# Layer 1's MLP weight sums made during layer 0's MLP, three units behind the norm, and an earlier first down block

## Chip, cores and metric

One Trainium2 chip, one core of it. The metric is the device time of one execution in microseconds (us).

## What is computed

A two-layer diffusion backbone over 1024 latent tokens and 256 context tokens, D_MODEL 1024, D_FF 4096, in float32. Layer 0 mixes with a bidirectional mLSTM and a Fourier transform, layer 1 with differential attention and a convolution. Each layer ends with the part that the change touches:

```python
def squared_relu_mlp(h, w1, w2):
    return jnp.square(jax.nn.relu(h @ w1)) @ w2
...
        x = x + mod_l[2] * y_l
        x = x + mod_l[5] * squared_relu_mlp(modulate(rmsnorm(x, g_norm[l, 1]), mod_l[3], mod_l[4]), w_ff1[l], w_ff2[l])
```

Layer 0 runs the MLP on latent and context tokens, layer 1 on the latent tokens alone.

## The kernel before

**Arithmetic.** A float32 product is made of three matmuls: each operand is split into a rounded half `hi` and a rest `lo`. ACT makes `hi` (a cast), DVE makes `lo` (a subtraction). Weights come through a ring of three staging tiles `st` (128x1024 floats, 512 KB): SP loads one (L95), ACT casts it to `wah` or `wbh` (L108), DVE subtracts to `wal` or `wbl` (L109), and the tile is free again.

**Layer 0's MLP** (`mlp`, L728). The hidden size is done in blocks of three 128-wide hidden tiles. A block is an up phase (three tiles by three token blocks, `acc`, then Relu, Square and a split, L747 to L751) and a down phase (eight output tiles `fo` by three token blocks, `ff`, each added to the residual `x` by DVE at L708, with four banks for `ff`). Six weight loads feed a block, three of `ff1` and three of `ff2`. Beside the down phase runs `side`: layer 1's modulation vectors, made by DVE (L179, L181) from loads of `w_mod`, five or six to a block, through the same three `st` tiles.

**Layer 1's MLP** uses a seven-product scheme for 2x2 block matrices in place of eight products. Products are named by WORDER "1","5","6","3","7","2","4". The right-hand operands `B` are made from the normed activations behind the norm (`right1`, L1194): sums and differences by DVE and POOL, then a split. The left-hand operands are sums and differences of weight quarters. `left` (L1215) loads two `st` tiles, and makes the sums with four 128x512 additions on POOL for the up products (L1240 to L1244) and on DVE for the down products, then splits them (ACT L1224, DVE L1225). An up unit (`up_unit`, L1312) is 84 matmuls (seven products by four operand pairs by three) and covers two hidden tiles; there are 16. What the products give is gathered in four tiles of a ring `x` of eight (L1321 keeps a product, L1328 adds one). Units 0 to 13 store the right-hand operands of the down products to DRAM (`sw`), five of seven already split (NSPLIT 5); units 14 and 15 store plain tiles to `sd`. The first products "1" and "2" need only the unsummed half of the operands; units 0, 1 and 2 run them before and behind the norm's own matmuls, then `together` (L1300) interleaves units 0 and 1 for products 5, 6, 3, 7, 4, and unit 2 follows. The down products take the units' results in five blocks (DBLK, three units each, two in the last) by four pairs of output tiles. They begin after all 16 residual tiles `x` are reloaded from DRAM (L1127) and the first block's operands are loaded from `sw` (L1382, L1385).

**Order.** The kernel is written in this order, and a scheduler moves instructions within each engine's list. Each engine, SP's DMA queue among them, works through its list in order: an instruction that waits holds up all that stands behind it.

## Time and profile before

| | us |
|---|---|
| median of 3 runs (range) | 3122.47 (3122.32 to 3123.63) |
| profiled execution | 3123.65 |
| its span, first to last instruction | 3121.9 |
| PE busy | 2940.3 (94%) |
| DVE busy | 1997.1 (64%) |
| ACT busy | 1203.9 (39%) |
| POOL busy | 222.8 (7%) |
| DMA engines, mean rate | 120 GB/s |

The profiled execution took 1.75 us more than its span, and 1.18 us more than the median. The mean granted TensorE clock was 0.978 of full speed. Shares of a whole span hide stages with different limits, so stretches are read one by one below. Line numbers are those of the kernel before; the changed kernel has the same statements some lines later (L710 for L708, L111 for L109, L1311 for L1268).

### The profile page before, as it was taken

To read this page: it belongs to the slowest core of one execution; us is meant where nothing else is said; L and a number is where in the kernel's file an instruction comes from. 1 tells how busy PE (TensorE), PEld (TensorE's weight loads), DVE (VectorE), ACT (ScalarE), POOL (GpSimd) and SP (SyncE) were. 2 spreads that over 40 slices of the span, in tenths; PEclk is the share of its full clock that TensorE was granted. 3 is DMA by queue.
4 is the path that set the end of the run, shared out by engine and by line. 5 is a ranking of instruction groups with operands and counts; after the bars stand their busy time and mean duration, and the time that the engine had idled before them with its cause. 6 is when DMAs were issued, how large, how long until landed. Compare 5 with 4: busy or idle time off the path is not lost. (4 is left out here: it accounts for less than half of the span.)

```text
span 3121.9 us, 44126 instructions
## 1 busy us (share of the span) xinstructions
PE 2940.3 (94%) x16386; PEld 2463.2 (79%) x16386; DVE 1997.1 (64%) x3957; ACT 1203.9 (39%) x2660; POOL 222.8 (7%) x315
## 2 busy tenths in 40 slices
PE   6899999999999999999999798999999699969998
PEld 5787878788888888888888677877877577758787
DVE  5858696646454544444456687566677976647787
ACT  3335354433222222222242155566665545422222
POOL 0002011000000000000000000000001432300000
PEclk9999999999999999999999899999999899989999
DMA  6143334550122222222121433134432355585652
GB/s 213 45 154 111 110 112 140 179 166 28 41 75 75 82 68 81 82 68 75 55 84 54 140 97 104 58 96 126 157 98 102 134 210 206 202 298 177 235 170 75
DMA packets 231911, 373.22 MB, mean 120 GB/s; under 512 B 21536, under 2 KB 116368, under 8 KB 231696
## 3 DMA queue, kind: packets, MB, share of 16 engines
q1 hardware_dynamic: 229104, 366.47, 35.8%
q10 hardware_dynamic: 2592, 3.93, 0.4%
q8 instruction: 129, 2.11, 0.3%
q14 instruction: 86, 0.70, 0.1%
HBM read 283.95 MB, written 86.37 MB: 119 GB/s over the span
## 5 line engine op out<-in xcount | busy, mean ns | idle before, releaser
L127 PE MATMUL acc<-a,wah 128*128 128x512 f32 (+1 forms) x1736 | 642.3, 370 | 14.9 <-DVE rt L1000 14.2
L128 PE MATMUL acc<-a,wah 128*128 128x512 f32 (+1 forms) x1736 | 637.5, 367 | 0.0
L129 PE MATMUL acc<-a,wal 128*128 128x512 f32 (+1 forms) x1736 | 636.7, 367 | 0.0
L127 PEld LDWEIGHTS acc<-a,wah 128*128 128x128 f32 x1736 | 332.5, 192 | 61.4 <-DVE rt L1000 14.8
L129 PEld LDWEIGHTS acc<-a,wal 128*128 128x128 f32 x1736 | 332.2, 191 | 46.3 <-DVE wal L109 0.2
L128 PEld LDWEIGHTS acc<-a,wah 128*128 128x128 f32 x1736 | 332.6, 192 | 45.1 <-issue 0.5
L127 PE MATMUL ff<-s,wbh 128*128 128x512 f32 (+1 forms) x768 | 274.0, 359 | 0.0
L108 ACT CAST wah<-st 128x1024 fp32r<-128x1024 f32 (+4 forms) x121 | 117.2, 971 | 404.1 <-DMA st<-in_ff_dram 305.2
L128 PE MATMUL ff<-s,wbh 128*128 128x512 f32 (+1 forms) x768 | 272.3, 355 | 0.0
L129 PE MATMUL ff<-s,wbl 128*128 128x512 f32 (+1 forms) x768 | 271.6, 354 | 0.0
L708 DVE SCALAR_TENSOR_TENSOR x<-ff,mod,x 128x512 f32<-128x512 f32 (+1 forms) x264 | 173.3, 660 | 105.4 <-PE ff L129 103.4
L751 DVE TENSOR_TENSOR s<-s,s 128x512 fp32r<-128x512 f32 (+1 forms) x96 | 57.9, 603 | 285.0 <-ACT s L750 284.9
L109 DVE TENSOR_TENSOR wal<-st,wah 128x1024 fp32r<-128x1024 f32 (+4 forms) x121 | 135.4, 1121 | 117.8 <-ACT wah L108 117.8
L1050 DVE TENSOR_REDUCE mx<-S 128x1 f32<-128x512 f32 (+1 forms) x288 | 165.8, 595 | 69.1 <-PE S L1048 67.4
L1268 PE MATMUL bd<-a,wbh 128*128 128x512 f32 x480 | 153.5, 400 | 43.3 <-ACT wbh L1224 23.5
L1056 ACT ACTIVATE p<-S,nm 128x512 f32<-128x512 f32 (+1 forms) x288 | 176.1, 620 | 44.2 <-DVE nm L1053 43.9
L1048 PE MATMUL S<-K,Q 128*128 128x512 f32 (+1 forms) x576 | 163.5, 383 | 14.0 <-ACT p L1056 7.6
L127 PE MATMUL acc<-wah,a 128*128 128x256 f32 (+1 forms) x560 | 163.1, 292 | 6.9 <-ACT a L269 4.5
L127 PEld LDWEIGHTS ff<-s,wbh 128*128 128x128 f32 x768 | 144.8, 189 | 23.6 <-ACT s L750 0.4
L128 PEld LDWEIGHTS ff<-s,wbh 128*128 128x128 f32 x768 | 145.2, 189 | 20.6 <-issue 0.2
L129 PEld LDWEIGHTS ff<-s,wbl 128*128 128x128 f32 x768 | 144.9, 189 | 20.8
L128 PE MATMUL acc<-wal,a 128*128 128x256 f32 (+1 forms) x560 | 160.7, 288 | 0.0
(395 smaller groups left out, 5924.6 us busy)
## 6 DMA issues: line engine op xcount, KB each, us to landing
st<-in_ff_dram SPq DMA_DIRECT2D x103, 512.0 KB
a<-sw SPq DMA_DIRECT2D x112, 256.0 KB
st<-in_w_mod_dram SPq DMA_DIRECT2D x48, 512.0 KB
sw<-o SPq DMA_DIRECT2D x70, 256.0 KB
stm<-in_w_mod_dram SPq DMA_DIRECT2D x128, 128.0 KB
bc<-rb SPq DMA_DIRECT2D x30, 512.0 KB
sw<-x SPq DMA_DIRECT2D x56, 256.0 KB
st<-in_w_qk_dram SPq DMA_DIRECT2D x24, 512.0 KB
```

The lines of the kernel that those rows point to most:

```text
L108: act.copy(hi, v)
L109: dve.tensor_sub(lo, v, f(hi))
L127: pe.matmul(ps, lh, rh, start=first, stop=False)
L128: pe.matmul(ps, lh, rl, start=False, stop=False)
L129: pe.matmul(ps, ll, rh, start=False, stop=last)
L708: dve.scalar_tensor_tensor(xt, ps, mod[:, self.l, ch, fo, s:s + 1], xt, MUL, ADD)
L751: dve.tensor_sub(lo, r, f(hi))
L1048: pe.matmul(s_, Q[m][:, kind, qb * P:(qb + 1) * P], K[hh, m][:, a:a + n], start=(kind == 0), stop=(kind == 1))
L1050: dve.tensor_reduce(mx[:, i:i + 1], s_, AX, MAX)
L1056: act.activation(e[:, a:a + n], S[i], AF.Exp, bias=nm, accum_out=Z[:, m, i:i + 1])
L1268: pe.matmul(ps, l_, r_, start=bool(first) and j == 0 and i == 0, stop=j == n - 1 and i == 2, skip_group_check=True)
```

## The change

- **Sums.** A generator `wsums` makes all weight sums of layer 1 while layer 0's MLP runs: 60 steps, two at each `fo` of the down phases, so 16 to a block of the first three middle blocks and 12 in the fourth. A step loads two halves of 256 KB into an `st` tile, adds and subtracts in place with four dependent 128x256 operations on POOL, and stores 512 KB to DRAM, `su` for `ff1` (32 steps) or `sv` for `ff2` (28 steps).
- **Left operands.** `left` makes no sums. It loads seven quarter operands, four of them sums, and splits them: 1.75 MB to an up unit.
- **Three units.** Units 1 and 2 are made inside the last loop of the attention output projection (`out_part`), at `fo` 2 and 5, and `together` interleaves three units. `out_part` takes its weights through `wa` instead of `wb`.
- **Down.** NSPLIT goes from 5 to 3, so two more of seven operands are split when they are read and not when they are stored. The first down block has two units, not the last. The last up unit takes the product order LORDER; behind its products "2" and "6" the first block's operands are loaded, and behind "4" four residual tiles. The other residual tiles are reloaded pair by pair of output tiles (`reload_x`), and the next block's operands are issued at the last pair of a block.

```diff
-DBLK = ((0, 1, 2), (3, 4, 5), (6, 7, 8), (9, 10, 11), (12, 13))
+DBLK = ((0, 1), (2, 3, 4), (5, 6, 7), (8, 9, 10), (11, 12, 13))
 NWP = 14
 WORDER = ("1", "5", "6", "3", "7", "2", "4")
-NSPLIT = 5
+LORDER = ("1", "2", "6", "7", "4", "5", "3")
+NSPLIT = 3
+NO = 21
...
+                for _ in range(2):
+                    next(sums, None)
...
+    su = dram.tile([16, P, 4, KT // 2, P], F32, name="su")
+    sv = dram.tile([NWP, 2, P, 2, 2, 2, P], F32, name="sv")
...
+        def wsums():
+            for j in range(16):
+                for h in (0, 1):
+                    t = wp.tile([P, 1024], F32, tag="st", bufs=3, name="st")
+                    v = t.rearrange("p (i e n c) -> p i e n c", i=2, e=2, c=P)
+                    for i in (0, 1):
+                        sp.dma_start(v[:, i], A["ff1"][1, 2 * j + i].rearrange("p (e n) c -> p e n c", e=2)[
+                            :, :, 2 * h:2 * h + 2])
+                    wsum(v)
+                    sp.dma_start(su[j, :, :, 2 * h:2 * h + 2], t.rearrange("p (s n c) -> p s n c", s=4, c=P))
+                    yield
+            for j in range(NWP):
+                for h in (0, 1):
+                    t = wp.tile([P, 1024], F32, tag="st", bufs=3, name="st")
+                    for e in (0, 1):
+                        sp.dma_start(t[:, e * 512:e * 512 + 512], A["ff2"][1, 2 * j + e, :, h * 512:h * 512 + 512])
+                    wsum(t.rearrange("p (e n i c) -> p i e n c", e=2, i=2, c=P))
+                    sp.dma_start(sv[j, h], t.rearrange("p (e n i c) -> p e n i c", e=2, i=2, c=P))
+                    yield
+        def wsum(v):
+            a, b, c, d = v[:, 0, 0], v[:, 0, 1], v[:, 1, 0], v[:, 1, 1]
+            pool.tensor_add(d, c, d)
+            pool.tensor_sub(c, a, c)
+            pool.tensor_sub(a, d, a)
+            pool.tensor_sub(b, b, a)
...
+        def ops_of(qs, pl, tag, stage):
+            e = len(qs)
+            v = four(stage(), e)
+            for i, q in enumerate(qs):
+                load(q, v[:, i])
+            hi, lo = (four(pl.tile([P, 1024], F32R, tag=tag + x, bufs=3, name=tag + x), e) for x in "hl")
...
         ops = {}
-        f0 = raw(0)
-        ops["1"], ops["2"] = split(f0, wp, "wa")
+        ops["1"], ops["2"] = ops_of(("A11", "A12"), wp, "wa", st)
+        if not early:
+            yield ops
+        ops["5"], ops["6"] = ops_of(("S1", "S2"), pfw, "wb", ws)
+        if early:
+            yield ops
+        ops["3"], = ops_of(("S4",), pfw, "wb", st)
+        ops["7"], ops["4"] = ops_of(("S3", "A22"), wp, "wa", st)
         yield ops
-        if again:
-            f0 = raw(0)
-        f1, y = raw(1), four(pf.tile([P, 1024], F32, tag="ws", bufs=1, name="ws"))
-        eng.tensor_add(y[:, 0], f1[:, 0], f1[:, 1])
-        eng.tensor_sub(y[:, 1], y[:, 0], f0[:, 0])
-        ops["5"], ops["6"] = split(y, pfw, "wb")
-        eng.tensor_sub(f1[:, 0], f0[:, 0], f1[:, 0])
-        eng.tensor_sub(f0[:, 1], f0[:, 1], y[:, 1])
-        ops["3"], = split(f0[:, 1:2], pfw, "wb")
-        ops["7"], ops["4"] = split(f1, wp, "wa")
-        yield ops
-
-    def up_left(j, again):
-        def load(i, t):
-            sp.dma_start(t, A["ff1"][1, 2 * j + i].rearrange("p (e n) c -> p e n c", e=2))
-        return left(load, HK, pool, again)
+
...
-        out_part(fo, 1, 6, KT, pfw, "wb")
+        out_part(fo, 1, 6, KT)
         spill(fo, 1)
+        if fo in (2, 5):
+            lead.append(up_unit(len(lead), True))
     norm_later(res.tot[1], 512, res.bank, right1)
-    for j in (1, 2):
-        lead.append(up_unit(j, True))
-        lead[j].run("1", "2")
+    for u in lead[1:]:
+        u.run("1", "2")
     drain()
     for op in "56374":
-        together(lead[:2], op)
-    for u in lead[:2]:
+        together(lead, op)
+    for u in lead:
         u.store()
-    lead[2].run(*"56374")
-    lead[2].store()
-    for j in range(3, 16):
+    for j in range(3, 15):
         u = up_unit(j)
         u.run(*WORDER)
         u.store()
-    load_x(px, 0, "x", F32, x2)
-    load_x(ap_, 1, "a2", F32R, x2)
-    for blk in DBLK:
-        B = down_ops(blk)
+    u = up_unit(15, False, LORDER)
+    nxt = {}
+    for op in LORDER:
+        u.run(op)
+        if op == "2":
+            nxt.update(down_ops(DBLK[0], ("1", "5", "6", "3")))
+        elif op == "6":
+            d = down_unit(DBLK[0], 0, nxt)
+            nxt.update(down_ops(DBLK[0], ("7", "2", "4")))
+        elif op == "4":
+            reload_x(0)
+    u.store()
+    for i, blk in enumerate(DBLK):
+        right, nxt = nxt, {}
         for fo in range(0, KT, 2):
-            down_unit(blk, fo).run(*WORDER)
+            if i or fo:
+                d = down_unit(blk, fo, right)
+            if i == 0 and fo < KT - 2:
+                reload_x(fo + 2)
+            if fo == KT - 2 and i + 1 < len(DBLK):
+                nxt = down_ops(DBLK[i + 1])
+            d.run(*WORDER)
...
+    def reload_x(fo):
+        for k, tb in ((fo, 0), (fo + 1, 1), (fo, 1), (fo + 1, 0)):
+            pl, t, dt = (ap_, "a2", F32R) if tb else (px, "x", F32)
+            res.x[k, tb] = f(pl.tile([P, 512], dt, tag=t, bufs=8, name=t))
+            sp.dma_start(res.x[k, tb], x2[:, k, tb * 512:tb * 512 + 512])
```

SP's queue in a down phase of layer 0's MLP, before (`in_w_mod` are modulation loads, `in_ff1` and `in_ff2` the next block's weights):

```order
L95 DMA st_9260<-in_w_mod_dram 128x4x256
L95 DMA st_9303<-in_w_mod_dram 128x4x256
L95 DMA st_9342<-in_ff1_dram 128x1024
L95 DMA st_9348<-in_ff2_dram 128x1024
L95 DMA st_9449<-in_ff1_dram 128x1024
```

and in the changed kernel, the last four of a block's 16 sums:

```order
L97 DMA st_9358<-in_w_mod_dram 128x4x256
L887 DMA st_9366<-in_ff1_dram 128x2x256 x2
L887 DMA st_9374<-in_ff1_dram 128x2x256 x2
L890 DMA su_7097<-st_9366 512x1x256
L890 DMA su_7097<-st_9374 512x1x256
L97 DMA st_9417<-in_w_mod_dram 128x4x256
L887 DMA st_9423<-in_ff1_dram 128x2x256 x2
L887 DMA st_9431<-in_ff1_dram 128x2x256 x2
L890 DMA su_7097<-st_9423 512x1x256
L890 DMA su_7097<-st_9431 512x1x256
L97 DMA st_9472<-in_ff1_dram 128x1024
L97 DMA st_9478<-in_ff2_dram 128x1024
```

All 16 sums of a block, and its modulation loads, now stand in front of the next block's first weight load.

DVE at the end of that block, before (L109 makes the `lo` half of the next block's weights, L708 updates the residual):

```order
L708 SCALAR_TENSOR_TENSOR x_7317<-ff_9268,mod,x_7317 128x512
L181 SCALAR_TENSOR_TENSOR av<-st,sT,av 128x256
L109 TENSOR_TENSOR wal<-st,wah 128x1024
L708 SCALAR_TENSOR_TENSOR x_7325<-ff_9279,mod,x_7325 128x512
L708 SCALAR_TENSOR_TENSOR x_7333<-ff_9290,mod,x_7333 128x256
```

and in the changed kernel, where these are the block's last updates:

```order
L710 SCALAR_TENSOR_TENSOR x_7320<-ff_9439,mod,x_7320 128x512
L710 SCALAR_TENSOR_TENSOR x_7328<-ff_9450,mod,x_7328 128x512
L710 SCALAR_TENSOR_TENSOR x_7336<-ff_9461,mod,x_7336 128x256
L192 STREAM_TRANSPOSE sc<-lone 128x64
L194 TENSOR_TENSOR mod<-sc,vec 128x2 x2
L111 TENSOR_TENSOR wal<-st,wah 128x1024
L111 TENSOR_TENSOR wbl<-st,wbh 128x1024
L111 TENSOR_TENSOR wal<-st,wah 128x1024
```

Before, this split stood among the updates of the last output tile but one, and another three tiles further ahead; at the ends of three blocks all six splits now stand behind the last update.

PE behind layer 1's second norm, before (product "5" writes `bd`, product "6" `acc`; `a_23152` and `a_23164` are the first and last operand of "5"):

```order
L1268 MATMUL bd<-a_23164,wbl 128x512
L1268 MATMUL acc<-o,wbh 128x512 x2
L1268 MATMUL bd<-a_23152,wbh 128x512
L1268 MATMUL bd<-a_23153,wbh 128x512
L1268 MATMUL acc<-o,wbl 128x512
```

and in the changed kernel (`a_23658` is the first operand of "5"):

```order
L1311 MATMUL bd<-a_23670,wbl 128x512
L1311 MATMUL acc<-o,wbh 128x512 x2
L1311 MATMUL bd<-a_23658,wbh 128x512
L1311 MATMUL bd<-a_23659,wbh 128x512
L1311 MATMUL bd<-a_23658,wbl 128x512
L1311 MATMUL bd<-a_23658,wbh 128x512
L1311 MATMUL bd<-a_23659,wbh 128x512
L1311 MATMUL bd<-a_23658,wbl 128x512
```

Behind unit 0's product "5" and the first pair of its "6", which has to wait for its operand, the same operand of "5" now serves two more units instead of one.

## Rows read from the trace of the kernel before

**Rows 1.** Busy table by stretch: layer 0's MLP, up and down, then layer 1's MLP.
```profile
core 0: us, PE busy (x) PEld busy (x) DVE busy (x) ACT busy (x) POOL busy (x), PEclk, DMA share, GB/s
801.27:842.60 41.33, 41.33 (x218) 35.67 (x217) 12.07 (x22) 14.83 (x26) 0.00 (x0) 1.00 0.17 52
...
926.90:969.60 42.70, 42.70 (x257) 36.43 (x250) 33.20 (x77) 4.03 (x6) 0.00 (x0) 1.00 0.28 87
...
2405.50:2477.00 71.50, 47.92 (x181) 35.05 (x181) 62.84 (x70) 31.47 (x49) 37.14 (x24) 0.83 0.27 95
2477.00:2762.80 285.80, 272.44 (x1161) 216.89 (x1159) 188.19 (x245) 135.44 (x221) 77.85 (x49) 0.99 0.63 227
2762.80:2786.30 23.50, 0.03 (x1) 0.03 (x1) 6.61 (x12) 3.44 (x7) 0.00 (x0) 0.57 1.04 351
2786.30:3061.00 274.70, 271.87 (x1169) 219.49 (x1169) 211.20 (x325) 74.81 (x112) 0.00 (x0) 0.99 0.58 189
```

**Rows 2.** Waits of PE between 2380 and 3061 us: total, times, longest.
```profile
PE bd L1268 <- ACT wbh L1224: 23.5, 1, 23.5
PE acc L1268 <- ACT x L1321: 15.2, 11, 6.9
PE bd L1268 <- ACT a L1174: 9.5, 1, 9.5
```

**Rows 3.** Timeline, SP's DMA issues from 790 us: start, length, engine, line, count.
```profile
792.37 19.02 SPq L95 DMA_DIRECT2D st<-in_w_mod_dram  x5
```

**Rows 4.** Timeline, SP's DMA issues from 862 us: weight loads of the next block.
```profile
862.62 6.15 SPq L95 DMA_DIRECT2D st<-in_ff_dram  x2
```

**Rows 5.** Timeline, ACT from 862 us: the cast of the first of those loads.
```profile
866.09 1.05 ACT L108 CAST wah<-st 128x1024 fp32r<-128x1024 f32 x1 [22.03 <-DMA st<-in_ff_dram]
```

**Rows 6.** Groups of DVE by line in one block of layer 0's MLP, 801 to 885 us.
```profile
L181 DVE SCALAR_TENSOR_TENSOR av<-st,sT,av 128x256 f32<-128x256 f32 x19 | 9.1, 480 | 1.8 <-DMA st<-in_w_mod_dram 1.8
L751 DVE TENSOR_TENSOR s<-s,s 128x512 fp32r<-128x512 f32 (+1 forms) x9 | 5.4, 603 | 28.8 <-ACT s L750 28.8
L109 DVE TENSOR_TENSOR wal<-st,wah 128x1024 fp32r<-128x1024 f32 x2 | 2.5, 1226 | 0.3 <-ACT wah L108 0.3
```

**Rows 7.** Groups of POOL by line in layer 1's MLP, 2380 to 3061 us.
```profile
L1244 POOL TENSOR_TENSOR st<-st,ws 128x512 f32<-128x512 f32 x16 | 33.2, 2075 | 74.3 <-DVE wal L1225 52.5 <-ACT o L1365 21.8
L1243 POOL TENSOR_TENSOR st<-st 128x512 f32<-128x512 f32 x16 | 22.9, 1431 | 0.0
```

**Rows 8.** Groups of POOL by line, whole span: the one of 128x256.
```profile
L621 POOL TENSOR_SCALAR_AFFINE_SELECT E<-E 128x256 f32<-128x256 f32 x60 | 26.1, 458 | 108.5 <-ACT E L619 92.6 <-PE pu L589 15.7
```

**Rows 9.** Timeline of POOL, 2418 to 2447 us.
```profile
2426.14 2.27 POOL L1241 TENSOR_TENSOR ws<-ws,st 128x512 f32<-128x512 f32 x1
2428.37 1.27 POOL L1243 TENSOR_TENSOR st<-st 128x512 f32<-128x512 f32 x1
...
2443.03 3.38 POOL L1212 TENSOR_TENSOR x<-x 128x512 f32<-128x512 f32 x2
```

**Rows 10.** Timeline of DVE, 2440 to 2450 us.
```profile
2443.54 1.75 DVE L1178 SCALAR_TENSOR_TENSOR a<-a,mod,a 128x512 fp32r<-128x512 f32 x1
...
2448.74 0.74 DVE L1178 SCALAR_TENSOR_TENSOR a<-a,mod,a 128x512 fp32r<-128x512 f32 x1
```

**Rows 11.** Timeline of ACT, 2418 to 2447 us.
```profile
2428.44 1.04 ACT L1224 CAST wbh<-ws 128x1024 fp32r<-128x1024 f32 x1 [7.76 <-POOL ws L1241]
```

**Rows 12.** Timeline of PE, 2418 to 2447 us.
```profile
2430.06 0.80 PE L1268 MATMUL bd<-a,wbh 128*128 128x512 f32 x1 [9.51 <-ACT a L1174]
...
2444.35 1.22 PE L1268 MATMUL acc<-o,wbh 128*128 128x512 f32 x2 [6.88 <-ACT x L1321]
```

**Rows 13.** Timeline, SP's DMA issues where the down products start.
```profile
2762.41 3.45 SPq L1127 DMA_DIRECT2D x<-x  x7
...
2770.62 4.41 SPq L1382 DMA_DIRECT2D a<-sw  x7
...
2778.15 2.32 SPq L1259 DMA_DIRECT2D st<-in_ff_dram  x4
```

More of the change, by code (lines that the diff above doesn't have):

```diff
@@ L726, in norm2, with mlp @@
             norm_later(self.tot[tb], TBS[tb][1], self.bank, sink)
-    def mlp(res, pf, pw, p2, tbs, h2, segs, finish, pre, lead, side):
+    def mlp(res, pf, pw, p2, tbs, h2, segs, finish, pre, lead, side, sums):
         l = res.l
@@ L1203, in right1 @@
             dve.tensor_sub(x[k, 0], x[k + HK, 1], x[k, 0])
-        B["6"] = [osplit(po_, "o", 20, x[k, 0], shift(k + HK)) for k in range(HK)]
+        B["6"] = [osplit(po_, "o", NO, x[k, 0], shift(k + HK)) for k in range(HK)]
         B["3"] = [osplit(ap_, "a5", 32, x[k + HK, 1], shift(k + HK)) for k in range(HK)]
@@ L1209, in right1 @@
             pool.tensor_sub(x[k, 1], x[k + HK, 1], x[k, 1])
-        B["7"] = [osplit(po_, "o", 20, x[k, 1], db[:, k:k + 1]) for k in range(HK)]
+        B["7"] = [osplit(po_, "o", NO, x[k, 1], db[:, k:k + 1]) for k in range(HK)]
         for k in range(HK):
@@ L1213, in right1, with left, four @@
         B["4"] = [osplit(ap_, "a2", 8, x[k + HK, 0]) for k in range(HK)]
-    def left(load, n, eng, again=False):
-        def four(t):
-            return t[:, :2 * n * P].rearrange("p (e n c) -> p e n c", e=2, c=P)
-        def split(v, pl, tag):
-            e = v.shape[1]
-            hi, lo = (four(pl.tile([P, 1024], F32R, tag=tag + x, bufs=3, name=tag + x))[:, 0:e] for x in "hl")
+    def left(load, n, early=False):
+        def four(t, e):
+            return t[:, :e * n * P].rearrange("p (e n c) -> p e n c", e=e, c=P)
+        def ops_of(qs, pl, tag, stage):
[4 more added lines that the diff above has]
+            hi, lo = (four(pl.tile([P, 1024], F32R, tag=tag + x, bufs=3, name=tag + x), e) for x in "hl")
             act.copy(hi, v)
@@ L1226, in split, with st, ws @@
             return [(hi[:, i], lo[:, i]) for i in range(e)]
-        def raw(i):
-            t = four(wp.tile([P, 1024], F32, tag="st", bufs=3, name="st"))
-            load(i, t)
-            return t
+        def st():
+            return wp.tile([P, 1024], F32, tag="st", bufs=3, name="st")
+        def ws():
+            return pf.tile([P, 1024], F32, tag="ws", bufs=1, name="ws")
         ops = {}
-        f0 = raw(0)
-        ops["1"], ops["2"] = split(f0, wp, "wa")
-        yield ops
-        if again:
-            f0 = raw(0)
@@ L1254, in down_left @@
-    def down_left(blk, fo):
-        n, h = len(blk), 2 * blk[0]
-        def load(i, t):
-            for e in range(2):
-                sp.dma_start(t[:, e], A["ff2"][1, h + e:h + 2 * n:2, :, (fo + i) * P:(fo + i + 1) * P].rearrange(
-                    "h p c -> p h c"))
-        return left(load, n, dve)
+        ops["1"], ops["2"] = ops_of(("A11", "A12"), wp, "wa", st)
[4 more added lines that the diff above has]
+            yield ops
@@ new lines, in left, with up_left, load @@
+        ops["3"], = ops_of(("S4",), pfw, "wb", st)
+        ops["7"], ops["4"] = ops_of(("S3", "A22"), wp, "wa", st)
+        yield ops
+    SUMS = ("S2", "S4", "S3", "S1")
+    def up_left(j, early):
+        def load(q, t):
+            if q in SUMS:
+                src = su[j, :, SUMS.index(q)]
+            else:
+                src = A["ff1"][1, 2 * j + int(q[1]) - 1].rearrange("p (e n) c -> p e n c", e=2)[:, int(q[2]) - 1]
+            sp.dma_start(t, src)
+        return left(load, HK, early)
@@ L1296, in run @@
                 ps, first = self.bank(op)
-                product(ps, op, self.A, B, first)
+                product(ps, op, self.A, self.right, first)
                 self.finish(op, ps)
@@ L1307, in together, with up_unit @@
             for u, (ps, first) in zip(units, banks):
-                product(ps, op, u.A, B, first, (j,))
+                product(ps, op, u.A, u.right, first, (j,))
         for u, (ps, _) in zip(units, banks):
             u.finish(op, ps)
-    def up_unit(j, again=False):
+    def up_unit(j, early=False, order=WORDER):
         t = {}
@@ L1388, in down_ops, with down_unit @@
         return nb
-    def down_unit(blk, fo):
+    def down_unit(blk, fo, right):
         def upd(*to):
```

33 lines of the change are left out of this document (22 added, 11 removed).

## The prediction

> **What bounds the kernel now.** I read the page first: PE is busy 94% of the span, so a gain has to come from PE's idle time or from stretches at the lower of its two clocks (1.2 of 2.4 GHz), and a loss from making PE idle where it is not. So the second view is the busy table by stretch [rows 1]. In layer 0's MLP, where the sums go, PE is busy in all of every stretch, at full clock; POOL does nothing there, the DMA engines are 17 to 28% busy. That is the room the change counts on, and PE has no slack to give. An up phase of 41.33 us is 216 matmuls, 72 for each of the token blocks of 512, 512 and 256, or 180 of 512 in all: 0.2296 us for one. Up and down together make 84 us to a block.
>
> In layer 1's MLP three stretches lose time. Behind the norm (2405.5 to 2477) 181 matmuls should take 41.6 us and took 71.5: 30 us lost. The units up to 2762.8 are 1152 matmuls by the code (60 of unit 2, 13 units of 84), 264.5 us, and took 285.8: 21 us. The start of the down products is 23.5 us without a matmul, and the down products' 1176 matmuls, 270.0 us, took 274.7. Together 79 us: no more than this can be won. The list of PE's waits [rows 2] names them: one of 23.5 us for ACT's cast of the first down weights, one of 9.5 for a split operand of product "5", eleven of 15.2 in all for ACT's copy L1321.
>
> **What the sums cost in layer 0.** What limits them is not POOL's time but three staging tiles and SP's order: 16 sums stand in front of the next block's weights. Step by step:
> - A load: weights issued at 862.62 were cast at 866.09, so 3.5 us from issue to use [rows 4, 5]. A sum's load comes in two halves, the second issued 0.4 us after the first (an issue takes 0.5 to 0.6 by lengths and counts in [rows 13], with the DMA engines full; I take a little less): 3.9. A store of the same size is given 3.5.
> - A POOL operation: the nearest of its kind is 128x512 [rows 7, 9], 1.27 us at its shortest, 1.43 on average at L1243. Half the width halves the 1.27 to 0.64; what the mean lies above the least, 0.16, I leave whole, since it is waiting and not width. Dependent ones follow without a gap, as L1243 does with no idle time in front of it [rows 7]. 0.80 us, so 3.2 us to a sum. Ends: 0.46 us, the one POOL row of 128x256, with one input in place of two [rows 8], and 1.04, half of L1244's 2.08.
> - A round: two sums are loaded, POOL takes 3.2 us for each in turn, the second store is issued (0.4 us) and the next loads stand behind it; the first store, issued at 7.1, has landed by 10.6. The third tile goes to modulation loads. 3.9 + 6.4 + 0.4 = 10.7 us for two sums, 86 for 16.
> - Six weight loads through three tiles: two passes of 3.5, a cast of 1.05 [rows 5] and three splits of 1.23 [rows 6], 8.2 each, 16.
> - 102 us against 84: 18 us late in each of three blocks, 54. The fourth has 12 sums, 64 + 16 = 80, and is not late.
> - The lead: the first modulation load of this phase goes out at 792.37 [rows 3], 9 us ahead of the up phase at 801.27 [rows 1]. Less 9.
> - Three stalls of several us let the granted clock fall, as it did behind the norm, where the stretch with the long waits has a mean of 0.83 [rows 1]: 3 us, an estimate.
>
> **Layer 0 loses 48 us.** PE shows it at two places: in front of the next block's first product, since all six splits stand behind the block's last update, and inside the down phase, since DVE's modulation steps [rows 6] wait for loads that now stand behind sums, and the residual updates that free the four `ff` banks stand behind those steps.
>
> POOL and DVE hold each other up: L1178 took 1.75 us while POOL was at work and 0.74 a few us later; L1241 took 2.27 us where L1243 took 1.27 [rows 9, 10]. The Trainium skill speaks against the change here: "GPSIMD Engine Reference", section "Key points", says that GpSimd shares its SBUF interfaces with VectorE and contends with DVE instructions that have two SBUF inputs. By that rule the modulation steps and weight splits of [rows 6] would be held up beside the sums; the trace agrees as far as L1178 goes.
>
> **What layer 1 gains.**
> - Behind the norm. ACT's cast for product "5" stood behind a cast of weights that waited for POOL's sum until 2428.4 [rows 9, 11]; without that sum "5" starts 2 us earlier than 2430.06 [rows 12], at 2428. It then has three units to serve, 36 matmuls, 8.3 us, some of it at half clock: 2439. Product "6" waited until 2444.35 for a free tile of the ring `x` [rows 12]; 2 us earlier that is 2442. The other 144 matmuls take 33 us: 2475. Before, the third unit's 60 matmuls came behind 2477: 2490.8. That is 16 us. The 24 matmuls that fill gaps in the projection loop are no longer there to cover the norm's own chain: that evens out. But three units hold twelve tiles of a ring of eight, so one unit's product waits until another has stored: 4 us back, between the mean and the longest of the waits for L1321, 1.4 and 6.9 us [rows 2]; it could be nothing. And restarts at half clock, 2 us. Gain 10 (5 to 18).
> - Up units: 21 us lost in 13 units. POOL's sums go, and with NSPLIT 3 two casts and two subtractions per unit. The waits for L1321 are waits for ACT's and DVE's queues; I take under half, 9 (4 to 15). The extra loads (1.75 MB to a unit, in 20 us) fit beside a DMA share of 0.63.
> - Start of the down products: SP issued residual tiles until past 2762.41, seven in that row alone, then operands, and the weights only at 2778.15, with the DMA engines full [rows 1, 13]. Now 20 operand loads, four residual tiles and the weights are issued during the last up unit, about 7 MB; at the 351 GB/s of [rows 1] that is 20 us beside a unit of 20. Some of it will be late: 23.5, and 2 us for the restart at a granted clock that had a mean of 0.57 there (an estimate), less 4 still waited. Gain 22 (14 to 25).
> - Down products: DVE's sums go, a second split of two operands comes, seven quarter loads come for four: nothing, covered by PE at 99% busy and a DMA share of 0.58; without that cover at most the 4.7 us now lost there, either way.
>
> **Sum.** +48 − 10 − 9 − 22 = +7 us on the profiled execution's 3123.65, 3130.7; it ran 1.2 us above the median of 3122.47, so 3129.5 on a median. About 0.2% (6 us) is what a measurement of this kernel tells from no change.
>
> **Rivals.**
> 1. *The sums fit.* A POOL operation of 0.46 us makes a round 3.9 + 3.7 + 0.4 = 8.0 us, a block 64 + 16 = 80 us, under 84: nothing accumulates, and only the splits behind the last update cost some 4 us at three block ends, 12. Then 3123.65 + 12 − 41 − 1.2 = 3093.5. It decides from 0.52 us an operation down (16 + 8 rounds of 4.3 + 8 × 0.52 = 84). For it: POOL idles here and PE needs few of DVE's two-input steps in an up phase. Against it: every 128x512 row is over 1.2 us. The Trainium skill's "GPSIMD Engine Reference", section "Elementwise — side-by-side cycle accounting", gives 2.6 cycles an element for two inputs at 1.2 GHz, by which 256 elements would be an estimated 0.55 us, this rival's side; the trace's 1.27 us for 512 is above that figure.
> 2. *POOL and DVE serialise.* At 1.04 us a round is 3.9 + 8.3 + 0.4 = 12.6, a block 101 + 18 = 119 with slower splits: 35 us three times, 10 in the fourth block (76 + 18), less 9, and 3 of clock: 109 us, 3190.5. Half-way from 48 to that, 78 us, gives 3159.5. DVE's rows beside POOL speak for it [rows 10], the plain mean of L1243 against it.
> 3. *The down start stays.* The operands need tiles that the last unit frees late, and the queue is only moved: gain 4 in place of 22, 3147.5. For it: 7 MB at the full rate take as long as the unit. Against it: the residual tiles that stood in front of the weights are now four.
> 4. *Layer 1 wins its upper ends*, 18 + 15 + 25, 17 more than forecast: 3112.5. For it: all of this is time that PE stood idle. Against it: every step has its own next wait.
>
> **Chances.** Forecast 0.42, its own range 3115 to 3143; rival 1 0.24; rival 2 0.15; rival 3 0.09; rival 4 0.10. Slower: 0.22 of the forecast's, all of rivals 2 and 3: 0.46. Same: 0.14 of the forecast's, 0.03 of rival 4: 0.17. Faster: rival 1, 0.07 of rival 4, 0.06 of the forecast's: 0.37. The range takes in rival 1 and the half-way price of rival 2: 3093 to 3160; what lies beyond it, with the ends of both, I hold for under 2 in 10.
>
> **What would show it.** Right: PE idle in 850 to 1140 us, at the ends of three blocks and in their down phases, some 15 to 20 us to a block, waiting for DVE (`wal`, `x`); SP's weight loads of these blocks late, behind `su` stores; POOL's 128x256 near 0.80 us. Layer 1's MLP from the end of the projection loop 41 us shorter; the 23.5 us wait under 5. Wrong: blocks of 84 us as before, or a POOL operation under 0.52; a down start above 10 us.

## The result, and the profile after

| | before | changed |
|---|---|---|
| median | 3122.39 us (3120.81 to 3123.63) | 3215.51 us (3212.63 to 3218.71) |
| ratio, 95% interval | | 1.0299 (1.0281 to 1.0317) |
| span of the profiled execution | 3121.9 us | 3210.9 us |
| mean granted TensorE clock | 0.978 | 0.963 |
| start of layer 1's MLP (first of its 2520 matmuls) | 2383.4 us | 2507.3 us |

The change is 3% slower, where +7 us (0.2%) was forecast. The whole loss stands ahead of layer 1's MLP: it starts 123.9 us later, ends 89.1 us later, and so wins 34.8 us itself. Layer 0 was forecast at +48, layer 1 at -41.

The first lines of the page after:

```profile
span 3210.9 us, 44648 instructions
PE 2956.2 (92%) x16386; PEld 2479.8 (77%) x16386; DVE 1960.8 (61%) x3877; ACT 1207.9 (38%) x2660; POOL 310.4 (10%) x491
```

The busy table by stretch after, over the up phase and the down phase (with the gap behind it) of each of the four blocks that carry the sums, and over one block behind them:

```profile
core 0: us, PE busy (x) PEld busy (x) DVE busy (x) ACT busy (x) POOL busy (x), PEclk, DMA share, GB/s
800.08:841.50 41.42, 41.42 (x218) 35.77 (x217) 14.69 (x22) 14.82 (x26) 21.58 (x28) 1.00 0.59 191
841.50:923.43 81.93, 46.65 (x265) 38.52 (x263) 30.91 (x68) 2.25 (x4) 28.50 (x37) 0.79 0.49 158
923.43:966.70 43.27, 43.27 (x217) 37.20 (x218) 21.91 (x30) 18.54 (x29) 20.07 (x26) 0.96 0.66 212
966.70:1036.98 70.28, 44.28 (x250) 37.13 (x248) 27.51 (x58) 2.25 (x4) 29.23 (x39) 0.85 0.56 179
1036.98:1078.50 41.52, 41.52 (x206) 35.54 (x207) 16.56 (x22) 17.99 (x29) 14.02 (x18) 0.97 0.65 215
1078.50:1154.43 75.93, 51.59 (x277) 42.59 (x275) 31.92 (x68) 2.73 (x5) 34.55 (x44) 0.80 0.49 167
1154.43:1196.00 41.57, 41.57 (x203) 35.40 (x204) 15.67 (x21) 17.60 (x28) 16.50 (x21) 0.96 0.64 216
1196.00:1261.32 65.32, 47.62 (x248) 40.06 (x246) 26.77 (x47) 4.08 (x7) 23.21 (x31) 0.87 0.59 198
1261.32:1345.40 84.08, 84.08 (x458) 71.88 (x457) 38.16 (x66) 22.34 (x35) 0.00 (x0) 1.00 0.24 75
```

Before, every such stretch was full of PE work [rows 1]. Now the up phases still are; the four down phases have 44 to 52 us of PE work in 65 to 82. Up start to up start the four blocks take 123.3, 113.6, 117.5 and 106.9 us where they took 84: +124.8 us. The block without sums is back at 84. PE's work itself takes 357.9 us in the four blocks where it took 336.4: the granted clock has a mean of 0.79 to 0.87 in the down phases. POOL is busy for a third to a half of these stretches and the DMA engines for 49 to 66%: neither is full.

Who waits, 800 to 1262 us after: two of PE's rows, then DVE's two on modulation loads, then SP's queue, in front of the sums' stores and in front of a sum's load (us in total, times, longest):

```profile
PE ff L129 <- DVE x L710: 81.5, 7, 20.4
PE acc L129 <- ACT wah L110: 18.4, 3, 9.9
...
DVE av L181 <- DMA st<-in_w_mod_dram: 86.3, 5, 24.7
DVE av L183 <- DMA st<-in_w_mod_dram: 37.5, 8, 10.1
...
SPq L890 <- POOL st L906: 98.2, 32, 3.9
SPq L898 <- POOL st L906: 89.3, 28, 5.0
...
SPq L887 <- DVE wbl L111: 12.9, 2, 10.6
```

This is the chain that the prediction named: SP stands in front of a store until POOL is done, modulation and weight loads stand behind it, DVE stands in its queue for those loads, and the residual updates that free PE's `ff` banks stand behind DVE's wait.

How long the sums take, from the timelines of SP (from 864 us) and POOL:

```profile
866.89 1.20 SPq L887 DMA_DIRECT2D st<-in_ff_dram  x2
874.03 0.56 SPq L890 DMA_DIRECT2D su<-st  x1
877.26 2.50 SPq L887 DMA_DIRECT2D st<-in_ff_dram  x4
885.04 3.64 SPq L890 DMA_DIRECT2D su<-st  x2
888.73 0.62 SPq L97 DMA_DIRECT2D st<-in_w_mod_dram  x1
889.41 3.52 SPq L887 DMA_DIRECT2D st<-in_ff_dram  x4
898.77 3.70 SPq L890 DMA_DIRECT2D su<-st  x2
903.73 0.38 SPq L97 DMA_DIRECT2D st<-in_w_mod_dram  x1
904.22 1.92 SPq L887 DMA_DIRECT2D st<-in_ff_dram  x3
```
```profile
870.83 0.74 POOL L903 TENSOR_TENSOR st<-st 128x256 f32<-128x256 f32 x1 [7.21 <-DMA st<-in_ff_dram]
...
873.27 0.74 POOL L906 TENSOR_TENSOR st<-st 128x256 f32<-128x256 f32 x1
881.89 0.72 POOL L903 TENSOR_TENSOR st<-st 128x256 f32<-128x256 f32 x1 [7.88 <-DMA st<-in_ff_dram]
...
895.05 0.89 POOL L903 TENSOR_TENSOR st<-st 128x256 f32<-128x256 f32 x1 [6.95 <-DVE av L183]
```

Follow one sum: its load goes out at 866.89 and POOL starts at 870.83 (3.9 us); POOL ends at 874.01 (3.2); the store goes out at 874.03, and only at 877.26, when a tile has come free, do the next loads go out (3.2). That is 10.4 us for **one** sum. Then two in 12.2 (877.26 to 889.41) and two in 14.8 (889.41 to 904.22). Over the four blocks the mean is 7.2, 6.2, 6.2 and 6.1 us a sum, from a block's first load for a sum to the first load behind its last one; the forecast's round gave 5.35.

POOL's groups for these stretches, 800 to 1262 us:

```profile
L904 POOL TENSOR_TENSOR st<-st 128x256 f32<-128x256 f32 x60 | 48.2, 803 | 4.7
L906 POOL TENSOR_TENSOR st<-st 128x256 f32<-128x256 f32 x60 | 46.0, 766 | 4.7
L183 DVE SCALAR_TENSOR_TENSOR av<-st,sT,av 128x256 f32<-128x256 f32 x75 | 43.3, 578 | 38.0 <-DMA st<-in_w_mod_dram 37.5
```

The four operations average 766 to 803 ns and follow one another within 0.08 us (4.7 us over 60). DVE's modulation step went from 480 [rows 6] to 564 to 578 ns on average: 858 in the 22 steps that had a POOL operation beside them for nine tenths of their time or more, 477 in the 83 that had none.

In layer 1, each matmul of the products set beside the one with the same count in the trace before shows where the 34.8 us come from: 6.9 us over the first 336 (units behind the norm), 16.6 from there to the 1344th (up units), 9.1 from there to the 1596th (start of the down products), 2.2 behind it. PE's waits there, 2480 to 3160 us after:

```profile
PE bd L1311 <- ACT wbh L1262: 8.8, 1, 8.8
PE acc L1311 <- ACT x L1364: 8.6, 3, 7.4
...
PE bd L1311 <- ACT a L1209: 2.8, 1, 2.8
```

The wait of 23.5 us [rows 2] is gone, and 24.4 us were won by the 1428th matmul, but one of 8.8 us ends at 2901.5, at product "5" of the last pair of output tiles in the first down block, with slower stretches around it: 15 us of the 24 are given back there.

### The profile page after: what moved, and what is told of

Its sections match the earlier page's. It is cut to its first block, busy times and chain, and to the rows that moved or that the text cites. A ratio compares the mean times of both kernels' runs of the same rounds, so it can differ in the third digit from the quotient of the medians.

```text
span 3210.9 us, 44648 instructions
## 1 busy us (share of the span) xinstructions
PE 2956.2 (92%) x16386; PEld 2479.8 (77%) x16386; DVE 1960.8 (61%) x3877; ACT 1207.9 (38%) x2660; POOL 310.4 (10%) x491
## 4 chain that ended last, share of the span: by engine, by line
PE 67%; DMA 12%; DVE 9%; POOL 6%; issue 3%; ACT 2%; SPq 1%; POOLq 0%; DVEq 0%; ACTq 0%
PE acc L131 9%; PE acc L129 9%; PE acc L130 9%; PE acc L1311 9%; PE bd L1311 7%; DMA st<-in_ff_dram 4%; PE ff L129 3%; PE po L1109 3%; PE ff L130 3%; PE ff L131 3%; PE S L1083 3%; DMA kd<-rh 2%; DMA qd<-rh 2%; PE pT L1104 2%; DMA su<-st 1%
## 5 line engine op out<-in xcount | busy, mean ns | idle before, releaser
L129 PE MATMUL acc<-a,wah 128*128 128x512 f32 (+1 forms) x1752 | 652.2, 372 | 36.8 <-ACT wah L110 21.9
L130 PE MATMUL acc<-a,wah 128*128 128x512 f32 (+1 forms) x1752 | 646.3, 369 | 0.0
L131 PE MATMUL acc<-a,wal 128*128 128x512 f32 (+1 forms) x1752 | 643.4, 368 | 0.0
L129 PEld LDWEIGHTS acc<-a,wah 128*128 128x128 f32 x1752 | 337.2, 192 | 87.1 <-ACT wah L110 25.9
L130 PEld LDWEIGHTS acc<-a,wah 128*128 128x128 f32 x1752 | 337.4, 193 | 45.6 <-issue 0.5
L129 PE MATMUL ff<-s,wbh 128*128 128x512 f32 (+1 forms) x768 | 280.8, 368 | 81.5 <-DVE x L710 81.5
L130 PE MATMUL ff<-s,wbh 128*128 128x512 f32 (+1 forms) x768 | 277.7, 362 | 0.0
L129 PEld LDWEIGHTS ff<-s,wbh 128*128 128x128 f32 x768 | 148.9, 194 | 108.6 <-DVE x L710 84.4
L130 PEld LDWEIGHTS ff<-s,wbh 128*128 128x128 f32 x768 | 149.4, 194 | 21.1 <-issue 0.2
```

Of the source, the lines that this page charges most:

```text
L129: pe.matmul(ps, lh, rh, start=first, stop=False)
L130: pe.matmul(ps, lh, rl, start=False, stop=False)
L131: pe.matmul(ps, ll, rh, start=False, stop=last)
```

## The experiments

Theory at the outset: the sums do not fit a block. Rivals: the extra bytes crowd the DMA engines; POOL and DVE hold each other up; POOL's work itself is too slow; SP's queue or the three staging tiles alone are at fault. The runs e1, e2, e7 and e8 leave out the weight sums (e2 only their four operations), so their time is that of the moves that are left.

**Where the loss is.** e1 puts a copy of the same size, from DRAM to DRAM, in the place of each sum; e2 takes only POOL's operations out.

```diff
e1: - t = wp.tile(...); sp.dma_start(v[:, i], ...); wsum(v); sp.dma_start(su[...], t...)
    + sp.dma_start(su[...], A["ff1"][1, 2 * j + h]...)
e2: - wsum(v)
```

> The 60 sums are replaced by 60 copies from DRAM to DRAM of the same bytes (512 KB read, 512 KB written each) on the same queue at the same places; no staging tile, no POOL work. The layer-1 weight sums are left out: what layer 1 loads is plain weights, of the same size. Theory A (the loss is a chain of latencies through SP's queue and the three staging tiles, with modulation and weight loads behind it): layer 0's blocks return to 84 to 87 us and the time falls by about 115 to 125 us from 3215.5, to 3088 to 3100, which shows layer 1's gain alone (35 us by the traces). Theory B (the DMA engines are too busy, loads become slow): the bytes are the same, so blocks stay over 105 us and the time over 3170. Theory C (POOL and DVE hold each other up at their memory port): as A here.

> The four POOL operations of each sum are left out; loads into the staging tiles and stores stay. Theory A: a sum's turn loses the 3.3 us of POOL but keeps the load (5 us in the trace) and the store's return; a round of two goes from 14.5 to about 9.5 us, a block to 8 x 9.5 + 18 = 94 us, so some 30 to 45 us of the 124 stay: 3120 to 3140. Theory B: no change, over 3190. Theory C: the loss goes altogether, 3085 to 3095.

e1: 3092.96 us, 0.9902 (0.9887 to 0.9916); blocks of 84 us. So layer 1's parts alone are worth about 30 us, and all that the change loses is in the sums. It is no test of bandwidth: a copy waits for no tile, and the scheduler moved all 60 to between 49 and 256 us, well ahead of layer 0's MLP. The first 16 in e1's timeline of SP:

```profile
49.53 24.46 SPq L882 DMA_DIRECT2D su<-in_ff_dram  x16
```

Bandwidth is excluded otherwise: in the changed kernel the DMA share is 0.49 to 0.66 in the blocks with sums and reaches 0.95 to 0.97 later (2838 to 2881 us), and e2 moves the same bytes in shorter blocks, at a share of 0.66 to 0.71.

e2: 3127.02 us, 1.0014 (1.0005 to 1.0023), blocks of 94.0, 99.6, 94.3 and 88.8. Of the 122.6 us between e1 and the change, loads and stores through the tiles make 34; POOL's operations, which lie between load and store, make 88.

**Half the pace, other queues.** e3 makes one sum for each `fo`; e4 issues loads and stores from POOL, e5 the stores only; e6 is e3 and e5 together.

```diff
e3: - for _ in range(2): next(sums, None)
    + next(sums, None)
e4: sp.dma_start -> pool.dma_start for the loads (v[:, i], t[...]) and stores (su, sv) of wsums
e5: sp.dma_start -> pool.dma_start for the stores (su, sv) only
```

> One sum at each output tile of the down phase instead of two: the same 60 sums over 7.5 blocks instead of 3.75, 8 to a block. Theory A: a block's queue holds 8 x 7 us of sums and 18 of weights, 74 us, under 84, so nothing accumulates; some waits for modulation loads stay in the first four blocks. Loss 5 to 30 us instead of 124: 3095 to 3120, faster than the kernel before. Theory B: half the rate of bytes, so most of the loss goes too. Theory C: each sum holds DVE up as before wherever it stands, the loss stays near 100: over 3180.

> The loads and stores of the sums are issued by POOL and not by SP; tiles and additions stay. Theory A in its form 'SP's order': SP no longer stands still in front of a store, so weights and modulation loads are only held by tiles: loss 40 to 80 instead of 124, 3130 to 3170. Theory A in its form 'three tiles': the tiles are held as long as before, or longer since POOL cannot issue a load while it adds: loss 110 or more, over 3200.

> The changed kernel with the sums' stores alone issued by POOL, right behind its own additions; loads stay on SP, two sums at each output tile. SP's 187 us of waiting for POOL in front of stores go. Theory A, form 'SP's order' (SP standing still in front of stores holds back the modulation and weight loads): most of the loss goes, 3100 to 3140. Form 'three tiles' (a sum holds a tile some 12 us from its load to the end of its store, 16 sums, 6 weights and 5 to 6 modulation loads need about 310 tile-us where three tiles give 252 in 84 us): the loss goes down little, to 80 to 120, 3170 to 3215.

> One sum at each output tile and the stores issued by POOL. One sum at each output tile alone lost 44 us against the copies. Form 'SP's order': that loss falls under 15, 3095 to 3108. Form 'three tiles': with 8 sums a block needs about 210 of 252 tile-us, so what was lost was the order; the same 3095 to 3115. If neither holds and modulation loads are late because loads are slow beside the sums' traffic: 3125 to 3137 as without it.

e3: 3136.54, 1.0045 (1.0028 to 1.0061), above what was expected: eight blocks of 84.2 to 99.5 us. With half as many sums in a block, all 60 lose 44 us against e1 and not 123; but not nothing. That POOL and DVE hold each other up is too little for the loss: POOL's work is the same here, and in the change the 130 modulation steps beside the sums took 74.3 us of DVE in place of 62.3. e4: 3266.36, 1.0458; e5: 3232.02, 1.0355; e6: 3137.25, 1.0053. Freeing SP from its wait in front of the stores, alone, wins nothing; in e18, below, each such store takes 0.73 us of POOL and a wait in front of it.

**Tiles of their own.** In e9 the sums use six tiles that are idle in a down phase, so that `st` is left to weights and modulation; e10 is e9 with the old `DBLK` and two units behind the norm in place of three; e11 is e10 with one sum for each `fo`.

```diff
e9: - t = wp.tile([P, 1024], F32, tag="st", bufs=3, name="st")
    + t = f(wp.tile([P, 1024], F32R, tag=("wah", "wal")[h], bufs=3, name=("wah", "wal")[h]))
```

> The change with one edit: the sums are loaded into, made in and stored from six tiles of their own (wah and wal, which hold the up weights and are idle during a down phase), so that the three staging tiles st are left to modulation and weight loads; the DMA traffic, POOL's work and SP as the one issuing queue stay. Theory 'three staging tiles' (sums, weights and modulation loads want some 305 tile-us of a block's 252): blocks fall from 107-123 us to 84-92, time 3095 to 3125. Theory 'SP's order and the latency' (each store stands in SP's queue until POOL is done, and modulation and weight loads stand behind it, whatever tiles there are): blocks stay above 97 us, time above 3150.

> e9 with the two other parts undone that cost time with the copies: the old split of the down blocks (three units in the first, 17 us better there) and two units in place of three together behind the norm (5 us better there). If the parts add, e9 less 17 to 23 us. By the tile theory that is 3075 to 3105, below the kernel before and below the change; by the theory of SP's order above 3125.

> e10 with one sum for each fo in place of two, so that the sums spread over twice as many blocks. Tile theory: with tiles of their own the pace of the sums no longer decides, so within 10 us of e10. Theory of SP's order: half as many stores to stand before, so 10 to 40 us below e10.

e9: 3197.81, 1.0240 (1.0225 to 1.0255), blocks of 108 to 119: the tiles alone are not the cause, as the rival said. e10: 3186.72, 1.0205 (1.0188 to 1.0222), 11 us below e9 and not 17 to 23. e11: 3106.98, 0.9947 (0.9930 to 0.9965), 80 us below e10, more than either theory gave: what counts is how many sums a block has to hold.

**Tiles and queue together, and the order of the queues.** e13 is e9 with stores issued by POOL; e15 is e9 with each store behind the next sum's loads. e14 is the change with the modulation steps done first, at six for each `fo`, and the sums begun behind them; e17 is e14 with the next block's up weights loaded and split ahead of the sums; e18 is e17 with stores issued by POOL.

```diff
e13: e9, and sp.dma_start -> pool.dma_start for the stores
e15: + last()                                  # in front of each yield
     + last = partial(sp.dma_start, su[...], t...)
e14: + for _ in range(6): end = next(side, 0) == 0
     + for _ in range(2 * end): next(sums, None)
e17: + for hd in blocks[bi + 1]:               # ahead of "for fo in range(KT)"
     +     nw1[hd] = wload(A["ff1"][l, hd], (KT, P))
e18: e17, and sp.dma_start -> pool.dma_start for the stores
```

> e9 (the sums in six tiles of their own) and e5 (their stores issued by POOL) together. If tiles and SP's standing before stores bind together, so that either alone uncovers the other: blocks of 84 to 95 us, 3095 to 3130. If neither is the cause (DVE standing at modulation loads, or the round trip of load and store): 3170 or above, as e9 alone.

> The change with one edit: the modulation steps go at six for each fo in place of three, and the sums begin only when the steps are done, in the later blocks, still two for each fo. Tiles, queue and rounds of the sums stay. If PE is stopped because DVE stands at modulation steps whose loads are behind the sums in SP's queue, then the blocks with sums lose only at the splits of the next block's weights: about 90 us each, 3100 to 3135. If the sums do not fit a block (16 at 6 us and the weights, 112 us): four blocks of 105 to 115 us still, 3180 to 3215. Twice as many modulation steps in the first blocks may cost up to 10 us by either.

> e9 with one edit: each sum's store is issued after the next sum's loads, so that a load is in flight while POOL adds. If the serial round is the cause, a sum takes about (4.3 + 3.2 + 0.5) / 2 = 4.0 us in place of 5 to 6, 16 of them and the weights 80 us in a block of 84: 3095 to 3125. If DVE's standing at modulation loads is the cause, most of the loss stays: 3150 to 3190.

> e14 with one edit: the three up weights of the next block are loaded and split before the down phase's sums and not behind them; sums, their rounds of 15 us for three and their bytes stay. If PE is stopped by DVE standing at these splits in front of the updates: the 73 us that PE waits for DVE's updates fall under 15, the four blocks with sums come to 84 to 92 us, 3100 to 3130. If the sums themselves do not fit into a block (16 sums at 5.1 us and six weights, about 100 us, whatever the order): the wait only moves to the down weights in front of the next down phase, 3150 to 3190.

> e17 with the sums' stores issued by POOL, so that SP goes on to the next free tile's load. If SP's rounds set the pace: a sum holds one of three tiles for 4.6 (load) + 3.2 (POOL) + 0.7 (issue) + 4.0 (landing) = 12.5 us, so 4.2 us a sum, 16 take 67 and the weights 16, 83 us in a block of 84: the 81 us that PE waits in e17 fall under 30, 3100 to 3135. If the hold on three tiles is longer than that (the pace stays at 5 to 6 us): 3165 to 3190, as e17.

e14: 3188.86, 1.0216 (1.0201 to 1.0231). The last two blocks with sums take 113 us with no modulation load in the way. Those loads are thus not the main cause: the kernel takes 27 us less without them in between, and the rest of the loss stays. Its timelines of SP, DVE and PE show one such block:

```profile
1392.98 3.85 SPq L896 DMA_DIRECT2D st<-in_ff_dram  x6
1401.95 6.55 SPq L898 DMA_DIRECT2D sv<-st  x3
1408.55 3.37 SPq L896 DMA_DIRECT2D st<-in_ff_dram  x6
...
1423.48 1.26 SPq L896 DMA_DIRECT2D st<-in_ff_dram  x2
1424.78 1.60 SPq L97 DMA_DIRECT2D st<-in_ff_dram  x2
```
```profile
1431.35 1.23 DVE L111 TENSOR_TENSOR wal<-st,wah 128x1024 fp32r<-128x1024 f32 x1 [32.30 <-ACT wah L110]
1432.49 2.46 DVE L710 SCALAR_TENSOR_TENSOR x<-ff,mod,x 128x512 f32<-128x512 f32 x4
```
```profile
1433.29 0.58 PE L129 MATMUL ff<-s,wbh 128*128 128x256 f32 x1 [27.81 <-DVE x L710]
```

Three sums make a round of 15.6 us (1392.98 to 1408.55) and the next of 14.9. The weight whose load goes out at 1424.78 is split in DVE's queue **in front of** residual updates; DVE stands there for 32.3 us, and PE 27.8 us for the updates behind it.

e17 takes this split out of the way: 3184.47, 1.0197 (1.0180 to 1.0214). The wait for updates is gone, all of it, and as the second theory said it comes back elsewhere. PE's and ACT's wait in e17, 700 to 1800 us, and the busy table over a down phase and the up phase behind it:

```profile
ACT wbh L110 <- DMA st<-in_ff_dram: 285.2, 13, 69.2
...
PE acc L129 <- ACT s L749: 81.6, 4, 26.4
```
```profile
1390.48:1432.00 41.52, 41.52 (x219) 35.72 (x218) 17.52 (x26) 2.15 (x4) 21.88 (x29) 1.00 0.59 189
1432.00:1501.50 69.50, 43.07 (x218) 36.82 (x217) 11.86 (x14) 18.30 (x30) 26.18 (x36) 0.80 0.51 175
```

A down phase of 41.5 us and an up phase of 69.5: 111 us again. Now the down weights are late. ACT stands 69.2 us in front of its cast of one of them, until 1461.97, and its work on the up products (L749), which frees PE's `acc` banks, stands behind that cast; DVE's splits of these weights stand in front of the activations' splits in the same way. **The place of the wait is set by the order in the queues of DVE and ACT; its length is set by what 16 sums and six weights take.**

e18: 3170.64, 1.0158 (1.0141 to 1.0175), not the 3100 to 3135 of the first theory but in the range of the second: blocks of 102 to 106 us. POOL in e18:

```profile
1302.90 0.81 POOL L907 TENSOR_TENSOR st<-st 128x256 f32<-128x256 f32 x1
...
1307.11 0.73 POOL L894 DMA_DIRECT2D su<-st  x1 [0.95 <-POOL st L910]
1307.79 0.81 POOL L907 TENSOR_TENSOR st<-st 128x256 f32<-128x256 f32 x1
```

A sum takes 4.9 us here: 3.2 of operations, 0.73 of issuing the store and 1 us between the last operation and the issue, and POOL makes ten in a row without waiting for a load. Over a whole turn of SP's queue it does wait. From the first weight load at 1336.31 to that of the next block at 1442.02 the six weights hold the queue for 21.2 us and the 16 sums for 84.5, or 5.3 each, and POOL stands for 38 of the 105.7 us until a load is there. e13 (3169.19, 1.0149, 1.0134 to 1.0165) and e15 (3167.10, 1.0140, 1.0123 to 1.0157) missed their 3095 to 3125 or 3130 too. (e15 lies in the range of its second theory, but e14 leaves that theory's cause no more than 27 us.) In e13 SP issues the next block's first weight load at 878.94, behind ten sums since 838 us, and DVE stands at its split, with residual updates behind it, for 18.2 us:

```profile
886.18 1.23 DVE L111 TENSOR_TENSOR wal<-st,wah 128x1024 fp32r<-128x1024 f32 x1 [18.20 <-ACT wah L110]
```

So e13 and e15 quicken the rounds and keep the order, e17 changes the order and keeps the rounds, and e18, which does both, still needs 106 us for 16 sums and six weights: POOL holds its pace in some of the rounds, the loads in others. A pace well under 4.9 us together with e17's order was not tried, so how much of the 124 us each is worth by itself stays open.

**Layer 1 by itself.** e7 is e1 with two units interleaved behind the norm, as before; e8 is e1 with the old `DBLK`; e12 is the kernel before with nothing but the early loads of the first down block, its sums made in each unit as before.

```diff
e7:  - together(lead, op)
     + together(lead[:2], op)          # the third runs behind them
e8:  - DBLK = ((0, 1), (2, 3, 4), ...)
     + DBLK = ((0, 1, 2), (3, 4, 5), ...)
e12: before + LORDER for the last up unit, down_ops and reload_x inside it
```

> The kernel with copies in place of sums (3093), with two units instead of three interleaved behind the norm and the third after them, as before the change. If three together win there, as the traces say (7 us up to product 336): 3096 to 3104. If the win came from the sums being gone alone: 3090 to 3096.

> The kernel with copies in place of sums (3093), with the down blocks of before (three units first, two last); the loads during the last up unit stay, 7.7 MB instead of 5. If the smaller first block is what shortens the start: the first wait grows by the 2.6 MB at 330 GB/s, 8 us, less the second wait of 8.8 us and its restart that came 40 us later: 3088 to 3097. If the start is hidden either way and the second wait goes: 3080 to 3088. If operands for three units do not fit their tiles while the last unit runs: 3100 to 3115.

> The kernel before with only one part of the change: the first down block's operands, residual tiles and weights loaded during the last up unit (in the order LORDER), with the old split of the blocks, and with the sums where they were, in each unit. Layer 0 keeps its 84 us blocks. If the down start alone is worth the 22 us that the prediction gave it: 3095 to 3105. If the wait of 23.5 us only moves (the second block's operands or the DVE sums come late in its place): 3112 or above.

e7: 3087.49, 0.9893 (0.9877 to 0.9910) against e1's 0.9902 (0.9887 to 0.9916): no difference that these runs can tell, so the third unit wins nothing. e8: 3075.80, 0.9857 (0.9842 to 0.9871): the smaller first block costs 14 us by the ratios and 17 by the medians, and e8 has no wait over 1.7 us in the down products. The next block's operands are issued at a block's last pair; with two units in the first block PE gets there sooner, and 16 of these loads stand in SP's queue ahead of the weights for that pair's product "5". SP after the change:

```profile
2876.32 9.44 SPq L1427 DMA_DIRECT2D a<-sw  x16
...
2895.10 0.95 SPq L1303 DMA_DIRECT2D ws<-sv  x2
```

e12: 3116.14, 0.9979 (0.9970 to 0.9988), 7 us and not 22. Its PE wait at the start of the down products:

```profile
PE bd L1269 <- ACT wbh L1225: 17.2, 1, 17.2
```

Loading early without ready sums leaves 17.2 of the 23.5 us: the operand of product "5" is a sum that needs the second pair of weights, and these are late again.

**The best version.** e16 is e11 with stores issued by POOL: tiles of their own, one sum for each `fo`, the old `DBLK`, two units behind the norm.

> e11 (3107) with the stores issued by POOL. e11 still has blocks of 87 to 95 us, about 35 us above 84 in all, and SP stands 122 us before its stores. If tiles and SP's standing bind together: 3075 to 3095. If POOL's issuing costs as much as SP's standing: 3105 to 3115.

3087.81 us, 0.9892 (0.9877 to 0.9908), as expected if tiles and queue bind together at this pace: 128 us below the change, 35 below the kernel before, with all sums made. Its four first blocks take 83.9, 91.5, 88.1 and 83.7 us, and PE's wait for updates in 700 to 1700 us is one twelfth of the change's:

```profile
PE ff L129 <- DVE x L710: 6.9, 6, 2.6
```

## Why the prediction was wrong

**The mechanism was right, the size was not.** The forecast said that the sums do not fit into a block, that weights and modulation loads would stand behind the stores, and that PE would wait for DVE in three blocks. It does, at the places named and in a fourth block too: 81.5 us for updates in the down phases, 18.4 for casts at the block starts. Forecast 48 us, measured 124. Some 21 us more went in PE's work at the lower granted clock (357.9 us for 336.4), where 3 were forecast; as SP's queue sets how long a block lasts, they are counted here as time in which PE would else have waited; no run tried this.

**The step that failed is the round**: "3.9 + 6.4 + 0.4 = 10.7 us for two sums, 86 for 16". Measured: 10.4 us for one, 12.2 and 14.8 for two, a mean of 6.1 to 7.2 us for each against 5.35. Three things went into it wrongly. A third tile that "goes to modulation loads" was one of three; at times such loads, with weights, held two, and the round had a single sum. Then the store's landing, which the forecast put beside the second sum's operations, has nothing beside it in such a round: the next load waits for the tile, and 3.2 us from store to load lie on the round in full. Last, the load was put at 3.9 us, which is its shortest: in the 34 sums for which POOL stood waiting it took 3.9 to 7.3, 5.0 at the median, and in the two rounds of two above 4.6 and 5.6 (877.26 to 881.89, 889.41 to 895.05). There the landing did lie beside POOL's work, all but 1.3 us (902.47 to 903.73). 16 × (7.2 - 5.35) + 32 × 0.85 + 12 × 0.7 is 65 of the 76 us between forecast and result.

**The lead did not come.** "Less 9" let the sums start ahead of the up phase. The first sum's load went out at 802.19, 2.1 us behind the start of the up phase at 800.08: SP had stood 10.6 us until DVE had split a weight and its tile was free. That is some 11 us, about the rest of the 76.

**The fourth block was not free.** "12 sums, 64 + 16 = 80, and is not late" lost 22.8 us: 12 sums at 6.1 us are 73, and in the blocks before it six weights took 13 to 23 us, not 16.

**POOL's operation was right**: 0.77 to 0.80 us measured, 0.80 forecast. Rival 1 (under 0.52) and rival 2 (1.04) are out. Rival 2's time was nearer, but its cause is not: POOL's operations stayed near 0.8, and DVE's modulation steps, which were held up, lost 12 us in all. The Trainium skill's "GPSIMD Engine Reference", section "Elementwise — side-by-side cycle accounting", gave an estimated 0.55 us by its 2.6 cycles an element. The trace agrees with that as a slope only: from 256 to 512 elements the least goes from 0.72 to 1.27 us [rows 9], 0.55 more, so by these two widths an estimated 0.17 us comes to each operation whatever its width.

**Layer 1**, -41 forecast, -34.8 measured: near, but by terms that missed in both directions. Behind the norm 6.9 for 10: the wait of 9.5 us for product "5" [rows 2] came down to 2.8, and one of 7.4 for L1364's copy stays; e7 shows that the third unit adds nothing to it. Up units 16.6 for 9: of the waits for L1321's copy, 15.2 us in eleven [rows 2], 8.6 us in three are left, 7.4 of it one wait behind the norm. Down start 9.1 for 22: the wait of 23.5 went as forecast, but the smaller first block brought one of 8.8, "its own next wait" of rival 4; e8 shows that the block split is its cause. e12 shows that it is the ready sums and not the early loads that remove most of the first wait.

With layer 0 at its measured 123.9 and layer 1 at 34.8 the sum is 3123.65 + 123.9 - 34.8 - 1.2 = 3211.6 us, 4 us under the median measured.

## What to carry to other kernels

Price a side job by its whole round as it stands in the issuing queue: load, wait, work, store and the store's landing until the tile can be loaded again, times the pieces that one stretch has to hold; the busy shares of POOL and of the DMA engines, a third to two thirds here, say nothing about it. Then look at what stands behind each piece in every queue: SP's order made the weights late, the order in DVE's and ACT's queues decided which of PE's products paid, and a change of either order alone moved the wait. Where the job does not fit its cover, spread it over more of it first: half the pace was worth 80 us (e10 to e11), tiles of its own 18 us (e9), and these together with another queue for the stores 46 (e13).

## What the runs showed of the hardware

A load of 512 KB in two halves took 3.9 to 7.3 us from its issue to POOL's first operation beside other transfers (median 5.0, the 34 sums of the change for which POOL stood waiting), and the time from a store's issue to the reuse of its tile was 2.6 us (1096.80 to 1099.43) to 4.9 (898.77 to 903.73, when the next load of that ring went out), 3.2 at the median. The Trainium skill's "DMA: Bandwidth & Descriptors", section "Anatomy of one DMA — SWDGE (gpsimd) path", gives 2.0 us and the bytes at 436 GB/s for a DMA that gpsimd issues, an estimated 3.2 us for 512 KB. The loads and stores here were issued by SP; the stores lie about that figure, the loads above it.

A store issued by POOL cost POOL 0.74 us for `su` and 0.58 for `sv` on average, and 0.7 and 0.4 us of standing in front of it (e18). In the same three tiles with weights and modulation loads, moving the stores there won nothing (e5, e6); with tiles of their own it won 29 us (e9 to e13) and 19 (e11 to e16), and behind the modulation steps, with the up weights ahead, 14 (e17 to e18).

Beside a POOL operation DVE's modulation step took 858 ns in place of 477; its residual update of 128x512, which reads `ff`, took 743 to 745 ns with POOL at work beside it or not.
